# Transformer layer with a Strassen-type feed-forward: the gate row on the tensor engine, group results emptied in small pieces, first splits spread over a projection

## The chip, the core and the metric

The kernel runs on one core of a Trainium2 chip. The core has a tensor engine (PE in the profile; its weight loads are listed as PEld), a vector engine (DVE), a scalar engine (ACT), GpSimd (POOL) and a sync engine (SP). PE writes its sums to eight PSUM banks of 128 x 512 floats. SP and GpSimd each issue DMAs in their own order, and both share the core's 16 DMA engines. The metric is the device time of one launch in microseconds: 2732.56 us, the median of three runs (2732.09 to 2735.61).

## What is computed

One layer over 512 latent tokens of width 2048, all in fp32: an adaptive layer norm, one combined input projection, a recurrent and a windowed-attention group of heads, an output projection with a gated residual, and a SwiGLU feed-forward of width 5632 with a gated residual. What the change touches is the part from the output projection on:

```python
sh_m, sc_m, gt_m, sh_f, sc_f, gt_f = split(silu(c) @ w_mod + b_mod, 6)
x = x + gt_m * (concatenate([hg_lat, at_lat]) @ w_out)
h = modulate(rms_norm(x, norm_ffn_g), sh_f, sc_f)
gate, up = split(h @ w_gate_up, 2)
x = x + gt_f * ((silu(gate) * up) @ w_down)
```

`gt_f`, called the gate row below, is one row of 2048 numbers, a product of the vector `silu(c)` with a 2048 x 2048 block of `w_mod`, plus a bias. It is wanted only at the very end, where the feed-forward's result is scaled.

## The kernel before

**Products.** Every fp32 operand is split into a high part and a low part (`wh`/`wl` of a weight tile `wr`, `fh`/`fl` of a feed-forward tile `fx`, `mT` and `hT` with two parts each), and one product becomes three PE products, high x high, high x low and low x high (`mm3`). ACT makes the high part by a copy, DVE the low part by a subtraction, so each weight tile goes DMA, ACT, DVE, PE.

**Output projection.** `proj_a` multiplies eight 128-row pieces of the mixed heads (`mT`) with 512 columns of `w_out`, for the token tiles in `toks`, into one bank per token tile (`mm`); after each token tile of each pair of rows it calls `tick()`, and at the end `evac` (`add_gated`), which multiplies by the mixer's gate (`tm<-mm,gt_c` on DVE) and adds to `x`. There are two halves: rows of heads 8 to 15 first (`mT0`), for column blocks j = 0 to 3, then the other heads' rows (`mT1`), j = 0 to 3 again. In the second half the last block is done as two calls, tokens (0,1) and then (2,3). The mixed heads come through a DRAM buffer; `upto` loads them and splits them.

**Lanes.** `tick()` advances three lists of small tasks, which are so woven in between the projection's products: `lane` holds the remaining work on the recurrent heads (`gate_head`, whose last step per head is four PE transposes, `aux<-ident,gt`), and `mod_lane` holds four `mod_gate` tasks, one for each 512 numbers of the gate row. Each of them loads 4 MB of `w_mod` by SP in eight pieces (`m_w`), takes 16 DVE steps of multiply-and-add into `m_acc`, then one PE product of `m_acc` with ones (two passes), and writes 512 numbers to `gtf_d`. `lane.drain()` stands between the two halves and `mod_lane.drain()` after j = 2 of the second half: what is not done by then is done there, in a row. The order is fixed when the program is built; each engine runs its own list in that order.

**Feed-forward.** It runs as 22 groups of up products and 16 groups of down products, by a scheme of seven products for a 2 x 2 block product (`PRODUCTS`), with sums of blocks on both sides. A group has several steps (eight for up; for down `ENDS` says after which step each group ends, and a group goes on from the one four before it), a step has 42 PE products of 256 columns, and a group's seven results fill seven of the eight banks: p1, p2, p6, p7, q4, q5, p3 in that order. For each step DVE forms sums of the loaded weight blocks (`st_sums`, three instructions on `fx`), ACT copies the high part in two instructions (`fh`), and DVE subtracts for the low part (`st_low`, `fl`, 128 x 1792); all this is issued two steps ahead of the products. The first two steps' splits are made between the calls for tokens (0,1) and (2,3) of the projection. The first eight steps also turn the tokens into the left operand (`turn`, `form_sums`, `form_low`; the tiles `a`).

**Emptying a group.** `evac_up` and `evac_down` are generators, advanced at fixed places of the step loop. At a group's end ACT copies p1, DVE makes two sums with p2 and p6 (`big<-aux,big` and the like), then comes the next `st_low`, and then five sums in a row with p7, q4, q5, q5 and p3. The next group's products can go into a bank when the sum that reads it is done. `evac_up` later multiplies with SiLU, forms sums (`a_sums`), splits (`hl`) and stores the result to `sf_d` by GpSimd; the down groups read it back as `a`. For each of the last four down groups (b = `FIN`), GpSimd adds the DRAM partial result `y_d` by an accumulating DMA, DVE multiplies by the gate row's 512 numbers (`gtr`, one buffer, loaded by `prepare`), GpSimd adds `x1_d`, and the result goes out; for the last group the tile `z` holds that sum ready.

## Time and profile before

| what | value |
|---|---|
| median of three runs | 2732.56 us |
| the profiled execution | 2736.58 us, of which the trace's span is 2734.8 us |
| PE busy | 2535.5 us, 93% of the span |
| DVE busy | 2136.3 us, 78% |
| ACT busy | 1091.6 us, 40% |
| TensorE clock, mean share of full speed | 0.979 |
| DMA | 488.83 MB, 179 GB/s in the mean |

The stages, by PE's timeline: input projection and heads to about 1005 us; first half of the output projection to 1112.7; work on the heads until 1127.8; second half with j = 0, 1, 2 to 1201.0; the rest of the gate row to 1227.2; tokens (0,1) and (2,3) of j = 3 to 1258.8; norm and first turns to 1276.5; up products to about 2215; down products to 2705.2; the end, without PE, to 2734.8. PE is the busiest engine nearly everywhere, so the views to read are those of what PE waits for. All rows carry L131, the line of a helper that issues every instruction; work is told apart by its tiles, written out<-in. A row such as "1.54 <-DVE big" in brackets is idle time of the engine just before the instruction, and what ended it.

### The profile page before, as it was taken

Reading aid. Unit: us, or ns where it says so; the run is one execution under the profiler, and the core shown is the slowest. Engines: PE = TensorE matmul, PEld = TensorE weight load, DVE = VectorE, ACT = ScalarE, POOL = GpSimd, SP = SyncE. Lnnn points to the kernel's source line nnn. Section 1 sums busy time; section 2 is a strip of 40 time slices with the busy share of each in tenths; the row PEclk is TensorE's granted clock in tenths of the full one; section 3 lists DMA queues with packets and bytes.
Section 4 is the critical chain, followed back from the end, with each engine's and each line's share of the span. In section 5 each row is a group of like instructions: output and inputs, shape, how many; then the busy total and the mean of one; then the engine's idle time right before and its main releaser. Section 6 shows DMA issues by size and latency. Waiting matters only on the chain.

```text
span 2734.8 us, 44380 instructions
## 1 busy us (share of the span) xinstructions
PE 2535.5 (93%) x17119; PEld 2288.9 (84%) x17119; DVE 2136.3 (78%) x3666; ACT 1091.6 (40%) x1801; POOL 258.6 (9%) x448
## 2 busy tenths in 40 slices
PE   7999999999999999767999999999999989999994
PEld 4579888878788878556999999999999989999994
DVE  4478868787888876656888888888888887777775
ACT  4245444446333332224544444434444433333331
POOL 0000010000011110100000000000000022222201
PEclk9999999999999999888999999999999999999998
DMA  9978677751532354752344444454444486777766
GB/s 346 300 266 264 208 231 239 231 179 60 158 97 91 101 176 157 228 180 69 109 131 155 140 142 157 126 162 154 127 156 150 150 291 229 208 219 228 221 157 155
DMA packets 310165, 488.83 MB, mean 179 GB/s; under 512 B 20417, under 2 KB 177250, under 8 KB 309186
## 3 DMA queue, kind: packets, MB, share of 16 engines
q1 hardware_dynamic: 258528, 351.35, 40.5%
q0 software_dynamic: 38048, 122.00, 14.8%
q10 hardware_dynamic: 13378, 12.65, 1.4%
q8 instruction: 134, 2.20, 0.3%
q14 instruction: 77, 0.63, 0.1%
HBM read 414.08 MB, written 71.84 MB: 178 GB/s over the span
## 4 chain that ended last, share of the span: by engine, by line
DVE 29%; issue 26%; PE 23%; DMA 13%; ACT 7%; POOL 3%; SPq 0%; DVEq 0%; ACTq 0%; POOLq 0%
PE mm L131 17%; DVE fx L131 9%; PE aux L131 6%; DVE big L131 6%; DMA m_w<-in_w_mod_dram 5%; ACT fh L131 4%; DVE fl L131 4%; DVE m_acc L131 2%; DVE wl L131 2%; DMA wr<-in_w_in_dram 1%; DMA y_d<-big 1%; DMA big<-x_d 1%; DMA big<-y_d 1%; POOL a L131 1%; DVE hP L131 1%
## 5 line engine op out<-in xcount | busy, mean ns | idle before, releaser
L131 ACT ACTIVATE fh<-fx 128x768 fp32r<-128x768 f32 (+1 forms) x528 | 483.2, 946 | 814.5 <-DVE fx L131 747.8
L131 DVE TENSOR_TENSOR fl<-fx,fh 128x1792 fp32r<-128x1792 f32 x264 | 533.9, 2023 | 170.1 <-ACT fh L131 169.0
L131 PE MATMUL mm<-a,fh 128*128 128x256 f32 x2464 | 470.0, 283 | 12.4 <-DVE big L131 9.1
L131 PE MATMUL aux<-a,fh 128*128 128x256 f32 x2464 | 469.5, 283 | 10.3 <-DVE big L131 10.3
L131 DVE TENSOR_TENSOR fx<-fx 128x256 f32<-128x256 f32 (+1 forms) x816 | 417.4, 512 | 43.9 <-DMA fx<-in_w_down_dram 13.1
L131 PEld LDWEIGHTS mm<-a,fh 128*128 128x128 f32 x2464 | 381.2, 189 | 17.1 <-DVE big L131 8.3
L131 PEld LDWEIGHTS aux<-a,fh 128*128 128x128 f32 x2464 | 381.1, 189 | 14.8 <-DVE big L131 9.2
L131 ACT ACTIVATE wh<-wr 128x512 fp32r<-128x512 f32 x376 | 227.1, 627 | 307.6 <-PE mm L131 191.4
L131 PE MATMUL mm<-a,fl 128*128 128x256 f32 x1232 | 348.6, 283 | 0.0
L131 PE MATMUL aux<-a,fl 128*128 128x256 f32 x1232 | 348.4, 283 | 0.0
L131 DVE TENSOR_TENSOR wl<-wr,wh 128x512 fp32r<-128x512 f32 x376 | 250.4, 684 | 98.0 <-ACT wh L131 97.3
L131 PE MATMUL mm<-wh,hT 128*128 128x512 f32 x896 | 297.0, 400 | 4.1 <-ACT hT L131 3.0
L131 PE MATMUL aux<-fh,a 128*128 128x256 f32 x1232 | 267.5, 284 | 15.8 <-DVE big L131 15.6
L131 PE MATMUL mm<-fh,a 128*128 128x256 f32 x1232 | 267.4, 284 | 14.5 <-DVE big L131 13.4
L131 PE MATMUL mm<-hT,wh 128*128 128x512 f32 x768 | 248.3, 399 | 0.0
L131 DVE SCALAR_TENSOR_TENSOR m_acc<-m_w,c_col,m_acc 128x512 f32<-128x512 f32 x240 | 179.4, 747 | 66.5 <-DMA m_w<-in_w_mod_dram 64.1
L131 PEld LDWEIGHTS mm<-a,fl 128*128 128x128 f32 x1232 | 231.2, 188 | 0.0
L131 PEld LDWEIGHTS aux<-a,fl 128*128 128x128 f32 x1232 | 231.1, 188 | 0.0
L131 PEld LDWEIGHTS aux<-fh,a 128*128 128x128 f32 x1232 | 209.5, 190 | 20.0 <-DVE big L131 15.6
L131 PEld LDWEIGHTS mm<-fh,a 128*128 128x128 f32 x1232 | 209.3, 189 | 18.5 <-DVE big L131 13.1
L131 PEld LDWEIGHTS mm<-wh,hT 128*128 128x128 f32 x896 | 168.4, 188 | 55.5 <-issue 8.6
L131 PE MATMUL mm<-wh,mT 128*128 128x512 f32 x512 | 169.5, 408 | 15.5 <-DVE gsig L131 6.1
(274 smaller groups left out, 4110.1 us busy)
## 6 DMA issues: line engine op xcount, KB each, us to landing
fx<-in_w_gate_up_dram SPq DMA_DIRECT2D x352, 256.0 KB, 3.3
wr<-in_w_in_dram SPq DMA_DIRECT2D x144, 512.0 KB, 4.3
m_w<-in_w_mod_dram SPq DMA_DIRECT2D x128, 512.0 KB, 4.6
fx<-in_w_down_dram SPq DMA_DIRECT2D x176, 256.0 KB, 6.1
sf_d<-big POOLq DMA_DIRECT2D x44, 896.0 KB, 6.0
ring<-in_w_mod_dram SPq DMA_DIRECT2D x64, 512.0 KB, 8.8
a<-sf_d POOLq DMA_DIRECT2D x44, 512.0 KB, 10.3
wr<-in_w_out_dram SPq DMA_DIRECT2D x36, 512.0 KB, 4.5
```

The source lines that it names most:

```text
L131: r = f(*a, **k)
```

## The change

**1. The gate row by PE.** The four `mod_gate` tasks are gone. A row tile `c_pad` with `silu(c)` in the first of 32 columns is the stationary operand; `gate_rows(k)`, for k = 0 to 15, multiplies it with a 128 x 2048 block of `w_mod` (`gw`, 1 MB, three buffers, loaded on GpSimd's queue) by four column-tiled products of 32 x 512, all into one bank. Four of these stand in j = 2, four in the call for tokens (0,1), three in that for (2,3), and five behind it; then one DVE addition of the bias and four small writes to `gtf_d`.

**2. Emptying in small pieces.** Pieces of at most three instructions stand between `st_sums` and `st_low`, where before they stood behind `st_low`. The sum with p3 comes one step later than those with q4 and q5, and these come after the next step's `st_sums`. The low part of a step is made in two instructions where no emptying is under way. The movements after a down group are in a list of their own (`moves`); `prepare(j + 1)` is called as soon as the one buffer of `gtr` is free, and `z` is loaded at the start of the last group.

**3. First splits spread.** `st_sums`, `st_high` and `st_low` of the first two steps stand at several places inside the calls for (0,1) and (2,3).

**4. `ENDS`** gives the last groups 5, 5, 8, 7, 6 and 5 steps in place of 6, 6, 8, 7, 5 and 4.

The core of the diff:

```diff
-ENDS = (2, 3, 5, 6, 8, 9, 11, 12, 14, 15, 17, 18, 22, 22, 22, 22)
+ENDS = (2, 3, 5, 6, 8, 9, 11, 12, 14, 15, 16, 17, 22, 22, 22, 22)
...
-    for j in range(4):
-        mod_lane.add(mod_gate(j, 5 * D, gtf_d))
...
-    def st_low(i):
+    def st_low(i, parted=False):
...
+            for a, b in ((0, 3), (3, 7)) if parted else ((0, 7),):
+                dve.tensor_tensor(u.lo[:, a:b, :], u.x[:, 1 + a:1 + b, :], u.hi.bitcast(F32)[:, a:b, :],
+                                  op=ALU.subtract)
...
+    def gate_load(k):
+        if k < KC:
+            gws[k] = est.tile(gw, [P, D], F32, "gw", "gw", 3)
+            pool.dma_start(gws[k], w_mod[k * P:(k + 1) * P, 5 * D:6 * D])
+
+    def gate_rows(k):
+        if k == 0:
+            pg.append(aux_bank())
+        w = gws.pop(k)
+        for j in range(4):
+            pe.matmul(pg[0][32 * j:32 * j + 32, :], c_pad[:, k, :], w[:, 512 * j:512 * j + 512], start=(k == 0),
+                      stop=(k == KC - 1), tile_position=(0, 32 * j), skip_group_check=True)
+        gate_load(k + 3)
...
+            if j == 2:
+                gate_rows(s // 2)
...
-    mod_lane.drain()
...
-    proj_a(ws, list(range(8)), mT, (0, 1), 512, last)
-    for i in range(2):
-        st_sums(i)
-        st_high(i)
-    for i in range(2):
-        st_low(i)
-    proj_a(ws, list(range(8)), mT, (2, 3), 512, last)
+    def before(s):
+        gate_rows(4 + s // 2)
+        if s == 2:
+            st_sums(0)
+            st_high(0)
+        if s == 4:
+            st_low(0)
+        if s == 6:
+            st_sums(1)
+            st_high(1)
+
+    proj_a(ws, list(range(8)), mT, (0, 1), 512, last, before)
+
+    def before(s):
+        if s > 0:
+            gate_rows(7 + s // 2)
+        if s == 0:
+            st_low(1)
+
+    proj_a(ws, list(range(8)), mT, (2, 3), 512, last, before)
+    for k in range(11, KC):
+        gate_rows(k)
...
+    dve.tensor_tensor(g_row, pg[0], g_row, op=ALU.add)
+    for j in range(4):
+        pool.dma_start(gtf_d[0:1, 512 * j:512 * j + 512], g_row[32 * j:32 * j + 1, :])
...
         dve.tensor_tensor(t, r, p7, op=ALU.subtract)
+        yield
         dve.tensor_tensor(u1, t, q4, op=ALU.add)
+        dve.tensor_tensor(t, q5, t, op=ALU.subtract)
         dve.tensor_tensor(r, q5, r, op=ALU.subtract)
-        dve.tensor_tensor(t, q5, t, op=ALU.subtract)
+        act.activation(t, t, AF.Silu)
+        yield
+        xx = est.tile(xg, [P, 8, SC], F32, "big", "big", 4)
         dve.tensor_tensor(r, p3, r, op=ALU.add)
...
+    def move(j, b, c, gt):
+
...
         dve.tensor_tensor(c, c, gt[:, None, :].to_broadcast([P, 4, 512]), op=ALU.mult)
+        prepare(j + 1)
         pool.dma_start(c, rows_of(x1_d, j), accum_op=ALU.add)
...
+        advance(tail)
+        if not u.up and u.b == 0 and u.g < 2:
+            advance(tail)
+        st_low(i + 2, not tail and not g)
...
         if g:
-            next(g, None)
+            next(g)
             tail.append(g)
+        advance(moves)
```

What this makes of the engines' lists. PE, before: the place where the two halves of the output projection meet (`mT_9843` and `mT_9844` are parts of the first half, `mT_10824` of the second).

```order
L131 MATMUL mm<-wl,mT_9843 128x512
L131 MATMUL mm<-wh,mT_9844 128x512
L131 MATMUL aux<-ident,gt 128x128 x12
L131 MATMUL aux<-m_acc,ones 128x512
L131 MATMUL mm<-wh,mT_10824 128x512
L131 MATMUL mm<-wl,mT_10824 128x512
```

PE, after, at the same place (the second half is `mT_10763` and `mT_10764` here).

```order
L131 MATMUL mm<-wl,mT_9843 128x512
L131 MATMUL mm<-wh,mT_9844 128x512
L131 MATMUL mm<-wh,mT_10763 128x512
L131 MATMUL mm<-wl,mT_10763 128x512
L131 MATMUL mm<-wh,mT_10764 128x512
```

The twelve transposes of the last three heads and the product of `m_acc` no longer stand between the halves: the transposes stand as fours inside the first half, the last of them some 20 rows ahead of its end.

GpSimd's DMA list, after, from j = 2 to the end of the projection (`x_d` is the store of one finished block of x, 1 MB; `gw` the loads for the gate row; before, the only other entries here are loads and writes of the gate row's bias and result).

```order
L131 DMA x_d<-x_9833 128x4x512
L131 DMA gw<-in_w_mod_dram 128x2048 x3
L131 DMA x_d<-x_9834 128x4x512
L131 DMA gw<-in_w_mod_dram 128x2048 x7
L131 DMA x_d<-x_9835 128x4x512
L131 DMA gw<-in_w_mod_dram 128x2048 x2
L131 DMA gtf_d<-g_row 16x1x32 x4
```

The last two loads of the gate row stand behind the store of the last block of x, and the writes of the finished row behind them. On PE five groups of column-tiled products (`aux<-gw,c_pad_10777`, twenty in a row) now stand between the projection's last product and the first turn.

DVE, before, at the end of an up group: sums of the next weights, two sums with p2 and p6, low part, then p7, q4, q5, q5 and p3.

```order
L131 TENSOR_TENSOR fx<-fx 128x512
L131 TENSOR_TENSOR fx<-fx 128x256 x2
L131 TENSOR_TENSOR big<-aux,big 128x512
L131 TENSOR_TENSOR big<-mm,big 128x512
L131 TENSOR_TENSOR fl<-fx,fh 128x1792
L131 TENSOR_TENSOR big<-big,aux 128x512
L131 TENSOR_TENSOR big<-big,mm 128x512
L131 TENSOR_TENSOR big<-aux,big 128x512 x2
L131 TENSOR_TENSOR big<-mm,big 128x512
```

DVE, after, at the same place.

```order
L131 TENSOR_TENSOR big<-aux,big 128x512
L131 TENSOR_TENSOR big<-mm,big 128x512
L131 TENSOR_TENSOR fl<-fx,fh 128x1792
L131 TENSOR_TENSOR big<-big,aux 128x512
L131 TENSOR_TENSOR fx<-fx 128x512
L131 TENSOR_TENSOR fx<-fx 128x256 x2
L131 TENSOR_TENSOR big<-big,mm 128x512
L131 TENSOR_TENSOR big<-aux,big 128x512 x2
L131 TENSOR_TENSOR fl<-fx,fh 128x1792
```

The sums with q4 and q5 now stand behind the next step's sums of weights and ahead of its low part; the sum with p3 has moved one step further.

## Rows read from the trace of the kernel before

**Rows 1.** Stretches: us, then busy us (instructions) of PE, PEld, DVE, ACT, POOL; clock; DMA.

```profile
1020.00:1030.00 10.00, 10.00 (x44) 8.04 (x44) 7.05 (x14) 3.08 (x6) 0.88 (x2) 1.00 1.05 371
1113.00:1128.00 15.00, 4.26 (x15) 2.25 (x16) 10.41 (x17) 3.20 (x6) 1.88 (x3) 0.66 0.66 216
1153.00:1160.00 7.00, 5.66 (x15) 4.00 (x15) 6.96 (x12) 2.48 (x6) 0.00 (x0) 0.58 0.58 172
1160.00:1201.00 41.00, 41.00 (x179) 33.68 (x178) 18.98 (x29) 12.96 (x28) 1.54 (x2) 0.99 0.50 165
1201.00:1227.00 26.00, 1.91 (x4) 0.69 (x3) 14.62 (x21) 3.63 (x9) 1.87 (x3) 0.58 0.67 214
1227.00:1266.00 39.00, 26.09 (x98) 19.86 (x96) 24.74 (x47) 12.12 (x22) 1.31 (x2) 0.85 0.27 93
```

**Rows 2.** PE's waits from 1000 to 1280: total us, times, longest.

```profile
PE aux L131 <- DVE m_acc L131: 24.1, 1, 24.1
PE aux L131 <- DVE gt L131: 9.8, 3, 7.5
...
PE mm L131 <- DVE tm L131: 4.4, 2, 3.3
```

**Rows 3.** PE's timeline around one group of column-tiled products, early in the kernel.

```profile
120.59 0.63 PE L131 MATMUL mm<-wh,hT 128*128 128x512 f32 x2
121.15 1.06 PE L131 MATMUL aux<-ring,c_pad 128*32 128x512 f32 x8
122.14 0.50 PE L131 MATMUL mm<-wl,hT 128*128 128x512 f32 x1
```

**Rows 4.** DVE's timeline around the end of one up group.

```profile
1502.32 1.60 DVE L131 TENSOR_TENSOR fx<-fx 128x512 f32<-128x512 f32 x3
...
1505.59 2.02 DVE L131 TENSOR_TENSOR fl<-fx,fh 128x1792 fp32r<-128x1792 f32 x1
1507.52 0.68 DVE L131 TENSOR_TENSOR big<-big,aux 128x512 f32<-128x512 f32 x1
1508.30 0.69 DVE L131 TENSOR_TENSOR big<-big,mm 128x512 f32<-128x512 f32 x1
...
1510.70 1.60 DVE L131 TENSOR_TENSOR fx<-fx 128x512 f32<-128x512 f32 x3
1513.43 2.03 DVE L131 TENSOR_TENSOR fl<-fx,fh 128x1792 fp32r<-128x1792 f32 x1 [1.13 <-ACT fh L131]
```

**Rows 5.** The same table of stretches, for the up and the down products.

```profile
1340.00:2200.00 860.00, 840.75 (x6908) 832.28 (x6909) 750.94 (x929) 363.53 (x412) 48.91 (x53) 1.00 0.47 148
2200.00:2700.00 500.00, 463.85 (x3781) 454.89 (x3779) 390.94 (x479) 175.59 (x198) 109.27 (x138) 0.99 0.73 215
```

**Rows 6.** Waits of PE and of DVE from 1340 to 2200.

```profile
PE aux L131 <- DVE big L131: 10.3, 22, 0.9
PE mm L131 <- DVE big L131: 9.1, 21, 0.6
...
DVE fl L131 <- ACT fh L131: 91.3, 81, 1.1
```

**Rows 7.** PE's waits from 2200 to 2700.

```profile
PE aux L131 <- DVE big L131: 15.6, 17, 2.8
PE mm L131 <- DVE big L131: 13.4, 17, 1.6
```

**Rows 8.** The last PE product, and DVE's and GpSimd's timelines behind it.

```profile
2704.96 0.28 PE L131 MATMUL aux<-fh,a 128*128 128x256 f32 x1
...
2712.12 2.90 DVE L131 TENSOR_TENSOR big<-big,gtr 128x2048 f32<-128x2048 f32 x2 [6.82 <-DMA gtr<-gtf_d]
2723.32 0.69 DVE L131 TENSOR_TENSOR big<-big 128x512 f32<-128x512 f32 x1 [8.31 <-DMA big<-x_d]
...
2702.01 1.08 POOL L131 DMA_DIRECT2D gtr<-gtf_d  x1
...
2714.83 1.30 POOL L131 DMA_DIRECT2D big<-x_d  x1 [4.77 <-DVE big L131]
```

More of the change, by code (lines that the diff above doesn't have):

```diff
@@ L1459, in tile_block @@
                       op=ALU.mult)
+    dve.tensor_tensor(g_row, pg[0], g_row, op=ALU.add)
+    for j in range(4):
+        pool.dma_start(gtf_d[0:1, 512 * j:512 * j + 512], g_row[32 * j:32 * j + 1, :])
+    m_st.close()
+    r_st.close()
+    asets = ctx.enter_context(tc.tile_pool(name="asets", bufs=1, side="right"))
     sets, xa = {}, {}
@@ L1482, in form_sums @@
         if s < 8:
-            a_sums(xa[s])
+            for _ in a_sums(xa[s]):
+                pass
             act.activation(sets[s][0][:, 0:3, :], xa[s][:, 1:4, :], AF.Copy)
@@ L1520, in evac_up @@
         yield
-        dve.tensor_tensor(hl[1], xx[:, 1:8, :], hl[0].bitcast(F32), op=ALU.subtract)
-        for i in range(2):
+        for i, (a, b) in enumerate(((0, 3), (3, 7))):
+            dve.tensor_tensor(hl[1][:, a:b, :], xx[:, 1 + a:1 + b, :], hl[0].bitcast(F32)[:, a:b, :],
+                              op=ALU.subtract)
             pool.dma_start(sf_d[2 * g + i].bitcast(F32).rearrange("f p n -> p f n"), hl[i].bitcast(F32))
@@ L1533, in prepare @@
     def prepare(j):
+        gt = est.tile(fx, [P, 512], F32, "gtr", "gtr", 1)
+        pool.dma_start(gt, gtf_d[0:1, 512 * j:512 * j + 512].to_broadcast([P, 512]))
         z = None
         if j == 3:
[L1537 to L1545 removed]
+            z = zs[0]
             dve.tensor_tensor(z, z, gt[:, None, :].to_broadcast([P, 4, 512]), op=ALU.mult)
             pool.dma_start(z, rows_of(x1_d, j), accum_op=ALU.add)
[L1548 removed]
+        prepared[j] = gt, z
+    zs = []
     prepared = {}
@@ L1569, in evac_down @@
         yield
+        dve.tensor_tensor(t, r, p7, op=ALU.subtract)
         done(0, 1)
-        dve.tensor_tensor(t, r, p7, op=ALU.subtract)
+        yield
         dve.tensor_tensor(c21, t, q4, op=ALU.add)
+        done(1, 1)
+        dve.tensor_tensor(t, q5, t, op=ALU.subtract)
         dve.tensor_tensor(r, q5, r, op=ALU.subtract)
-        dve.tensor_tensor(t, q5, t, op=ALU.subtract)
+        done(1, 0)
+        yield
         dve.tensor_tensor(r, p3, r, op=ALU.add)
-        for h, n in ((0, 0), (1, 1), (1, 0)):
-            done(h, n)
-        if z is not None:
-            return
+        done(0, 0)
+        if z is None:
+            moves.append(move(j, b, c, gt))
+        yield
+    def move(j, b, c, gt):
         if b < FIN:
@@ L1637, in tile_block, with advance @@
         turn(s, 1)
-    form_sums(0)
-    form_low(0)
-    form_sums(1)
-    form_low(1)
-    tail = []
+    for s in range(2):
+        form_sums(s)
+        form_low(s)
+    tail, moves = [], []
+    def advance(gens):
+        for x in list(gens):
+            if next(x, gens) is gens:
+                gens.remove(x)
     for i, u in enumerate(steps):
@@ L1658, in tile_block @@
             next(g)
-        for x in list(tail):
-            if next(x, tail) is tail:
-                tail.remove(x)
-        st_low(i + 2)
+        advance(tail)
+        if not u.up and u.b == 0 and u.g < 2:
+            advance(tail)
+        st_low(i + 2, not tail and not g)
         if i < 8:
@@ L1665, in tile_block @@
         if g:
-            next(g, None)
+            next(g)
             tail.append(g)
+        advance(moves)
         if not u.up and u.b == FIN and u.first:
-            tail.append(prepare(u.g))
+            if u.g == 0:
+                prepare(0)
+            if u.g == 3:
+                zs.append(est.tile(xg, [P, 4, 512], F32, "big", "big", 4))
+                pool.dma_start(zs[0], rows_of(y_d, 3))
         reload(i)
-    while tail:
-        for x in list(tail):
-            if next(x, tail) is tail:
-                tail.remove(x)
+    while tail or moves:
+        advance(tail)
+        advance(moves)
 _INS = ["x", "c", "ctx", "c_ctx", "w_mod", "b_mod", "norm_mix_g", "norm_ffn_g", "w_in", "hg_lb",
```

37 lines of the change are left out of this document (18 added, 19 removed).

## The prediction

> **What bounds the kernel now.** I read the page's first part, then the table of stretches, then PE's waits in each stretch, and then the timeline of the engine that PE waits for. PE is busy in 93% of the span, so only its idle time and its slow time can be won. The stretches show where these are. Between the halves of the output projection PE works 4.26 of 15 us, in the rest of the gate row 1.91 of 26 us [rows 1]; the one is work on the last heads (DVE `gt`, 9.8 us of waits), the other one wait of 24.1 us for `m_acc` [rows 2]. In the up products PE works 840.75 of 860 us, in the down products 463.85 of 500 [rows 5]; nearly all that is missing are waits for the sums that free its banks, 10.3 + 9.1 us [rows 6] and 15.6 + 13.4 us [rows 7]. Behind the last product stand 30 us without PE.
>
> Why the banks come late is seen on DVE. In an ordinary step of the loop its three sums start at 1510.70, the low part at 1513.43, after a wait of 1.13 us for ACT's high part, and a low part takes 1.94: 4.67 us. At a group's end the same two and seven sums take from 1502.32 to 1510.70, 8.38 us [rows 4]. So DVE needs 8.38 + 7 x 4.67 = 41.1 us for an up group, and more where later pieces exceed the 1.13 us. PE's product takes 840.75/6908 = 0.122 us [rows 5], a group of 8 x 42 of them 40.9 us. DVE is a little slower than PE: it has no lead, and what stands last in its row is late at each group's end, by 19.4 us in some 21 groups.
>
> **The sum is made against the profiled execution**, 2736.6 us (span 2734.8 and 1.8 outside it), which is 4.0 above the median; at the end 4.0 comes off.
>
> **1. Between the halves.** The head transposes now stand inside the first half. DVE loses some 36 us of `m_acc` steps in the two halves, so the heads' chain should come earlier; the three fours stand about 50 products (12 us) apart. Of the 15 us [rows 1] some 2 us stay: -13. Ends: -15, and -8 if the last head is still late by as much as its single longest wait, 7.5 us [rows 2]. One product of `m_acc` with ones goes from the first half: -1.
>
> **2. j = 0 to 2.** At the end of j = 0 PE waited 4.4 us for `tm` [rows 2], which stood behind an `m_acc` step waiting for its load, and ran at a clock of 0.58 after it: 15 products took 5.66 us [rows 1], where the later stretch has 41.00/179 = 0.229 each, so 2.2 us more. Both go: -6.6. Four gate groups come in. A group of the same shape takes 1.06 us, and from the last ordinary product (second of the pair from 120.59) to the next (122.14) pass 1.09 us more than the usual spacing [rows 3], with about 0.1 more behind it: 1.2 us. Four: +4.8.
>
> A rule that speaks against this part: the Trainium skill, TensorEngine Tiling (Array Packing), Tiling Modes, says that changing the tiling mode drains the engine, and here it is changed 24 times. The row has the drains in it and they are small, some 0.1 us on each side, 2.4 us in all. If each change emptied the engine for as long as the first product behind the group lasts, 0.50 us [rows 3], it would be 12 us, and the forecast 10 later; the row bears out the rule but not that size, and I keep the row's.
>
> **3. Rest of the gate row.** The stretch 1201 to 1227 goes, with its product and its cold clock: -26. Nothing else was drained there.
>
> **4. Tokens (0,1) and (2,3).** They took 31.8 us for 96 products, which at 0.229 are 22.0; 9.8 us were cold clock (0.85 [rows 1]) and waits for the first splits, which blocked the weight tiles' low parts on DVE. These go; seven gate groups add 8.4. The loads are tight: from the start of j = 2 to the last group some 24 MB have to come or go (13.6 of `gw`, 6 of weights, 3 of stores, 1.6 of `fx`) in about 74 us, 330 GB/s. The most seen in a 10 us stretch is 371 [rows 1]. I take 3 us of waits: +1.6 in all, ends -4 and +7.
>
> **5. Before the first turn.** The last product used to be followed after 7.4 us by the first turn. Now five gate groups come between, and their last two loads stand on GpSimd's queue behind the store of the last block of x, which waits for DVE's last addition, about 2.5 us after the last product. Then 3.1 MB are under way, 8.5 us at 371 GB/s, and some 2 us for landing and the group: 14 us instead of 7.4, +6.5 (ends +3, if the store leaves the loads room, and +12). The norm and `diag` lie beside it. The finished row's four small writes hold back the first `a` tile, which takes over their place in memory; I put that at nothing, since the first turns cover it, and up to +3 if not.
>
> **6. Up products.** DVE's new group: at the end 1502.32 to 1505.59 (3.27), the low part 1.93, the sum with p7 0.78: 5.98. Next step: sums 1.52, three sums at 0.6 (1508.30 to 1510.70 are four), low part 1.94: 5.3. All later pieces are at most two short sums and fit into the 1.13 us wait for ACT [rows 4, 6]. 5.98 + 5.3 + 6 x 4.67 = 39.3 us against PE's 40.9. So DVE gains 1.6 us a group until it leads by as much as its buffers allow; from then on PE should find each bank free, with little to spare at q5. The ceiling is the 19.4 us; the first groups, where the forming of `a` leaves no lead, keep some 4: -15. Ends -5 and -19. The second instruction of a parted low part costs 0.05 us, where DVE has time.
>
> **7. Down products.** A group of six steps: 5.98 + 5.3 + 4 x 4.67 = 30.0 us on DVE against 252 products at 0.122, 30.8, on PE. The gain of a group is half as large and groups of two or five steps have none, so the lead comes back more slowly: of 29.0 us of waits 24 go, ends -12 and -29. The other 7 idle us of that stretch I leave.
>
> **8. The end.** Before: the last product starts at 2704.96; `gtr` is asked for at 2702.01 and awaited until 2712.12; the sum with `x1_d`, asked for at 2714.83, is there at 2723.32 [rows 8], 18 us after PE, and 11.5 us of DVE work and the last store follow. Now the partial result for `z` is loaded a group ahead, and `gtr` is asked for when the product of the last-but-one group is done, which can be some 10 us before PE ends, since that group now ends five steps before it. With the same 10 us for `gtr`, 2.3 for the product and 8.5 for the sum, `x1_d` is in about 10 us after PE ends: -8, ends -3 and -11.
>
> **Sum.** -13 - 1 - 6.6 + 4.8 - 26 + 1.6 + 6.5 = -33.7 up to the first turn; -15 - 24 - 8 = -47 behind it. 2736.6 - 80.7 = 2655.9, less 4.0: **2652 us**.
>
> **Rivals.**
>
> *A. The loops gain nothing.* DVE's step is set by the round from sums to ACT to low part, and a piece between them may push ACT's work as well, since ACT runs SiLU and the split of the result in the same row. Then the new group is as long as the old one, the waits of [rows 6, 7] stay, and 39 us are missing: 2691. For it: ACT is what DVE waits for, 91.3 us in 81 waits [rows 6]. Against it: ACT has 363.5 of 860 us to do [rows 5].
>
> *B. Slower: the banks of q4 and q5 come later than now.* Their sums now stand behind the next step's three sums of weights, 1.52 us later in the row. If DVE gets no lead, each of some 37 groups waits longer by that, and the old waits stay: +56. 2736.6 - 33.7 - 8 + 56 - 4 = 2747. It decides from 42/37 = 1.1 us per group on. For it: DVE has no lead now, and the down groups end every 30 us with a spare of under 1 us. Against it: a wait of PE gives DVE the lead that it lacks, so the loss should be paid once and not in each group, as long as DVE's round is the shorter one.
>
> *C. The gate row's loads bound the projection.* They share the DMA engines with the weight tiles. At 290 GB/s in place of 330 the 24 MB take 84 us, +10, and weight tiles late in their turn would leave PE cold, some 4 more: 2666. For it: in the stretch of 26 us in which hardly anything but `m_w` was loaded, 214 GB/s went over [rows 1]; against it: there two buffers limited it.
>
> The Trainium skill, DMA: Bandwidth & Descriptors, Queues, rings and completion order, says that a DMA engine takes packets from its queues in turn; by that the loads on GpSimd's queue would take their share from SP's weight tiles whenever both are full, which is what C describes. No row here shows the two queues full at once.
>
> *D.* The order of the lists shows that the change is made as told; that a part of it doesn't take place is no case of its own.
>
> **Chances.** Forecast 60%, with its own range 2625 to 2675 (the ends of the steps, most of which will not fall on one side together: -27 and +23); A 14%, C 15%, B 8%, and 3% for a result near the old time by a mixture of A and B. A measurement of this kernel can tell some 0.2% from no change, 5.5 us. The range is to leave out B and the outer part of the others: 2622 to 2694. Faster 0.89, same 0.03, slower 0.08.
>
> **What would show it.** The wait of 24.1 us and the two idle stretches should be gone, and the clock stay near 1.00 from 1020 on until the last product of the projection. Right: 11 to 17 us there between that product and the first turn. In the up products PE's waits for `big` under 6 us in all and the interval of two group ends 40.9; in the down products under 8. If DVE's wait for `fh` stays at 91 us while the bank waits stay too, A holds; if the longest bank wait at q4 or q5 is near 2.5 us all along, B. If PE waits for `gw` or for `wh` in j = 2 and j = 3, C. What would make the forecast wrong most of all is DVE's lead: all of 6 and 7 rests on it.

## The result and the profile after

The changed kernel takes 2639.39 us (median of four runs, 2634.27 to 2641.55) against 2734.09 us: a ratio of 0.9649, 95% interval 0.963 to 0.9668, 95 us faster. 2652 us was forecast, with 2625 to 2675 as the forecast's own range. The way there differs from the forecast more than the sum does. The table sets the profiled executions' traces side by side, by PE's starts: the first product of the output projection, its last one, the first turn, the first up and the first down product, the last product, the end of the span.

| stretch, us | before | after | measured | forecast |
|---|---|---|---|---|
| start to the output projection | 1006.7 | 1001.8 | -4.9 | 0 |
| both halves of the projection, with what stood between | 251.6 | 222.9 | -28.7 | -40.2 |
| last product to first turn | 7.8 | 15.5 | +7.6 | +6.5 |
| turns | 7.3 | 5.5 | -1.8 | 0 |
| up products | 941.3 | 914.8 | -26.5 | -15 |
| down products | 492.1 | 456.1 | -36.0 | -24 |
| behind the last product | 27.8 | 23.1 | -4.7 | -8 |
| span | 2734.8 | 2639.8 | -95.0 | -80.7 |

The projection gave less than forecast, the loops more. The stretches of the changed kernel's projection, from j = 2 on, with the columns of [rows 1] (us, busy us and instructions of PE, PEld, DVE, ACT and POOL, clock, DMA share, GB/s):

```profile
1157.00:1184.00 27.00, 27.00 (x134) 18.50 (x136) 10.09 (x15) 7.10 (x16) 2.94 (x5) 1.00 0.86 303
1184.00:1203.00 19.00, 16.45 (x81) 9.15 (x74) 9.49 (x14) 7.03 (x15) 2.88 (x5) 1.00 0.74 275
1203.00:1226.00 23.00, 19.63 (x83) 10.39 (x87) 12.39 (x18) 7.45 (x15) 1.59 (x3) 0.85 0.67 235
1226.00:1240.00 14.00, 5.64 (x36) 0.67 (x28) 4.73 (x19) 0.80 (x3) 1.81 (x3) 0.64 0.67 252
```

PE is busy throughout j = 2, but in j = 3 (from 1184) it idles 2.6 and 3.4 us, the clock falls to 0.85 and then to 0.64. What it waits for from 1000 to 1280, as in [rows 2]:

```profile
PE aux L131 <- DMA gw<-in_w_mod_dram: 9.3, 4, 7.0
...
PE mm L131 <- ACT wh L131: 3.5, 2, 2.4
PE mm L131 <- DVE tm L131: 2.7, 3, 1.5
```

The wait of 24.1 us for `m_acc` and the waits for `gt` are gone. New are waits for the gate row's own loads and for the weight tiles' high parts. PE's and GpSimd's timelines at the end of the projection:

```profile
1225.10 1.92 PE L131 MATMUL aux<-gw,c_pad 128*32 128x512 f32 x16
...
1235.89 1.94 PE L131 MATMUL aux<-gw,c_pad 128*32 128x512 f32 x8 [7.03 <-DMA gw<-in_w_mod_dram]
1238.38 1.93 PE L131 MATMUL aux<-gw,c_pad 128*32 128x512 f32 x8 [0.55 <-DMA gw<-in_w_mod_dram]
1240.24 4.73 PE L131 MATMUL aux<-diag,x 128*128 128x128 f32 x40
...
1227.82 0.77 POOL L131 DMA_DIRECT2D x_d<-x  x1 [4.75 <-DVE x L131]
1228.59 1.05 POOL L131 DMA_DIRECT2D gw<-in_w_mod_dram  x2
```

The five groups behind the last product (the row of 16 at 1225.10 is two of them) wait for their last two loads, issued at 1228.59 behind the store of the last block of x at 1227.82; the first of the two is in at 1235.89, and a group takes 1.9 us there in place of 1.06, in a stretch with a clock of 0.64. The first turn starts at 1240.24.

In the loops the waits are turned round. DVE's waits from 1310 to 2170 in the changed kernel, to be set beside [rows 6]:

```profile
DVE big L131 <- PE aux L131: 20.5, 10, 2.0
DVE big L131 <- PE mm L131: 20.5, 10, 2.0
DVE fl L131 <- ACT fh L131: 16.6, 63, 0.3
```

DVE waits for PE, 41 us in 20 groups, where PE waited for DVE; and its wait for ACT has fallen from 91.3 to 16.6 us. One group's end on DVE, for [rows 4]:

```profile
1705.21 1.60 DVE L131 TENSOR_TENSOR fx<-fx 128x512 f32<-128x512 f32 x3
1707.03 2.17 DVE L131 TENSOR_TENSOR fl<-fx,fh 128x768 fp32r<-128x768 f32 x2 [0.21 <-ACT fh L131]
1709.12 1.61 DVE L131 TENSOR_TENSOR fx<-fx 128x512 f32<-128x512 f32 x3
1712.77 0.69 DVE L131 TENSOR_TENSOR big<-aux,big 128x512 f32<-128x512 f32 x1 [2.05 <-PE aux L131]
...
1714.18 2.02 DVE L131 TENSOR_TENSOR fl<-fx,fh 128x1792 fp32r<-128x1792 f32 x1
1716.11 0.68 DVE L131 TENSOR_TENSOR big<-big,aux 128x512 f32<-128x512 f32 x1
1716.71 1.60 DVE L131 TENSOR_TENSOR fx<-fx 128x512 f32<-128x512 f32 x3
```

The row at 1712.77 carries it: DVE has reached the group's end 2.05 us before PE's result is there. PE's period of a group is 336 products at 200.00/1665 us, 40.4 us, so DVE's round, the time that its work for one group takes without waits for PE, is 38.3. The lines of the same 200 us stretch, before and then after:

```profile
1700.00:1900.00 200.00, 195.53 (x1608) 193.50 (x1607) 174.26 (x217) 83.84 (x97) 7.83 (x8) 1.00 0.45 141
```

```profile
1700.00:1900.00 200.00, 200.00 (x1665) 199.78 (x1664) 181.96 (x235) 91.00 (x100) 9.91 (x10) 1.00 0.48 148
```

Before, 57 products fewer (6.8 us at 0.120 each) were done in 200 us, though PE was idle for only 4.5. In this stretch the breaks cost PE about half as much again as the idle time that the trace shows; PE's starts, one group to the next, stood 41.8 us apart and stand 40.4 apart now. This is why the loops gained more than the waits in [rows 6, 7] promise.

The end, PE, DVE and GpSimd in the changed kernel, and PE's last row of before:

```profile
2616.70 0.28 PE L131 MATMUL aux<-fh,a 128*128 128x256 f32 x1
...
2616.02 2.29 DVE L131 TENSOR_TENSOR big<-big,gtr 128x2048 f32<-128x2048 f32 x1 [3.83 <-DMA gtr<-gtf_d]
...
2627.39 0.69 DVE L131 TENSOR_TENSOR big<-big 128x512 f32<-128x512 f32 x1 [6.29 <-DMA big<-x_d]
...
2612.48 0.57 POOL L131 DMA_DIRECT2D gtr<-gtf_d  x1 [10.75 <-DVE big L131]
```

```profile
2706.96 0.28 PE L131 MATMUL aux<-fh,a 128*128 128x256 f32 x1
```

`x1_d` is in at 2627.39, 10.7 us after the last product. Before, the last product starts at 2706.96 and not at 2704.96: the row in [rows 8] (and the end of the down products in the list of stages) is not the kernel's last, and the sum was in 16.4 us after the last one, not 18.

### The profile page after: what moved, and what is told of

Same layout as the page of the kernel before. It is cut to its first block, busy times and chain, and to the rows that moved or that the text cites. A ratio compares the mean times of both kernels' runs of the same rounds, so it can differ in the third digit from the quotient of the medians.

```text
span 2639.8 us, 44545 instructions
## 1 busy us (share of the span) xinstructions
PE 2531.1 (96%) x17239; PEld 2282.7 (86%) x17239; DVE 2105.6 (80%) x3691; ACT 1110.5 (42%) x1801; POOL 265.7 (10%) x466
## 4 chain that ended last, share of the span: by engine, by line
PE 68%; DVE 11%; DMA 10%; issue 6%; ACT 2%; POOL 1%; SPq 0%; DVEq 0%; ACTq 0%; POOLq 0%
PE mm L131 40%; PE aux L131 28%; DMA m_w<-in_w_mod_dram 3%; DVE big L131 2%; DVE m_acc L131 2%; DVE wl L131 2%; DVE fx L131 1%; DMA wr<-in_w_in_dram 1%; DMA fx<-in_w_down_dram 1%; DMA big<-x_d 1%; DVE fl L131 1%; DVE ce L131 1%; DMA gw<-in_w_mod_dram 1%; DVE a L131 1%; POOL rs_t L131 1%
## 5 line engine op out<-in xcount | busy, mean ns | idle before, releaser
L131 ACT ACTIVATE fh<-fx 128x768 fp32r<-128x768 f32 (+1 forms) x528 | 500.2, 952 | 734.5 <-DVE fx L131 209.8
L131 DVE TENSOR_TENSOR fl<-fx,fh 128x1792 fp32r<-128x1792 f32 (+2 forms) x333 | 543.8, 1635 | 36.3 <-ACT fh L131 34.6
L131 PE MATMUL mm<-wh,mT 128*128 128x512 f32 x512 | 171.4, 406 | 10.7 <-DVE gsig L131 4.0
L131 PE MATMUL mm<-wl,hT 128*128 128x512 f32 x448 | 179.5, 401 | 0.3 <-DVE wl L131 0.3
```

The lines of the kernel that those rows point to most:

```text
L131: r = f(*a, **k)
```

## The experiments

In all of them the comparison is with the kernel before, on the same chip. Kernels that share the projection's code differ there by up to 5 us from trace to trace (221.5 to 226.4), and in the start by up to 6 (995.8 to 1001.8); the up and the down products of kernels that share the loops repeat within 2.3. Inside the projection j = 3 is steadier: from its first to its last product of `mT` it takes 39.9 to 40.0 us in the six kernels that have it as in the changed one. The stretches of all traces, as above:

| kernel | to projection | projection | to turn | turns | up | down | end | span |
|---|---|---|---|---|---|---|---|---|
| before | 1006.7 | 251.6 | 7.8 | 7.3 | 941.3 | 492.1 | 27.8 | 2734.8 |
| after | 1001.8 | 222.9 | 15.5 | 5.5 | 914.8 | 456.1 | 23.1 | 2639.8 |
| loops only | 1005.1 | 249.2 | 7.9 | 7.6 | 914.5 | 454.6 | 22.9 | 2661.7 |
| projection only | 998.5 | 226.3 | 15.1 | 5.4 | 941.1 | 493.1 | 26.1 | 2705.5 |
| early q | 998.1 | 224.0 | 15.5 | 6.4 | 912.8 | 458.1 | 21.3 | 2636.2 |
| dose of 8 | 997.6 | 226.4 | 15.2 | 5.4 | 944.9 | 455.5 | 22.5 | 2667.6 |
| gate without loads | 996.3 | 218.0 | 7.7 | 7.0 | 914.4 | 454.8 | 22.9 | 2621.2 |
| gate earlier by four | 999.8 | 229.8 | 7.6 | 7.8 | 914.5 | 455.7 | 23.2 | 2638.5 |
| first splits at once | 995.8 | 231.3 | 15.5 | 6.3 | 916.7 | 454.8 | 22.4 | 2642.8 |
| low parts parted only | 1006.3 | 250.2 | 7.9 | 7.6 | 911.7 | 479.3 | 26.0 | 2689.0 |
| no parting | 999.1 | 221.9 | 15.5 | 6.5 | 915.3 | 459.2 | 23.1 | 2640.5 |
| old row at the end | 1001.2 | 221.5 | 15.5 | 6.3 | 914.7 | 468.4 | 21.6 | 2649.1 |
| gate first | 998.0 | 224.0 | 7.6 | 7.5 | 914.9 | 453.8 | 23.3 | 2629.1 |
| gate first, early fx | 999.4 | 223.8 | 7.6 | 7.0 | 914.5 | 454.6 | 22.4 | 2629.3 |

### Do the parts add?

"Loops only" puts the projection, the lanes and the first splits back to the kernel before and keeps the new emptying, `moves` and `ENDS`; "projection only" is the reverse.

```diff
 # loops only, against the changed kernel
+    for j in range(4):
+        mod_lane.add(mod_gate(j, 5 * D, gtf_d))
...
-                gate_rows(s // 2)
...
+    proj_a(ws, list(range(8)), mT, (0, 1), 512, last)
+    for i in range(2):
+        st_sums(i)
+        st_high(i)
```

> The projection, the gate row and the first splits are as in the kernel before; the emptying in pieces and the new group lengths are as in the changed kernel. Theory (DVE's shorter round makes the loops PE-bound by itself): from the first product of the up phase on it takes what the changed kernel takes there (26.5 us less in the up products, 36.0 less in the down products, 4.7 less at the end), so about 2667 us; bank waits of PE in the up products under 5 us. Rival (the loops gained because the projection left them a better start, a hot clock and early loads): half of that or less, 2700 us or more.

2663.78 us (2660.85 to 2665.39), ratio 0.9756 (0.9729 to 0.9784).

> The gate row by PE and the spread first splits are as in the changed kernel, the loops as in the kernel before. If the two parts add, this is 26 to 28 us faster than before, about 2706 us, with bank waits of 19 us in the up products and 29 in the down products as before. Rival (the loops also gain from what the projection leaves): 2690 us or less.

2705.80 us (2702.39 to 2708.13), ratio 0.9911 (0.9882 to 0.9939). Within that spread each stretch takes in either kernel what it takes in its parent, and the two gains, 64 and 22 us on their chip, add to 86, which their intervals, some 7 us to either side each, don't tell from 95. The loops do not gain from what the projection leaves.

### Is it DVE's round against PE's?

A dose of work on DVE, and nothing else:

```diff
         st_low(i + 2, not tail and not g)
+        if 8 <= i < 8 * N_UP:
+            v = steps[i + 2]
+            dve.tensor_tensor(v.lo[:, 6, :], v.x[:, 7, :], v.hi.bitcast(F32)[:, 6, :], op=ALU.subtract)
```

> The changed kernel with one further DVE subtraction of 128 x 256 (0.43 us alone, some 0.38 in a row) behind the low part of every step of the up phase, repeating a part of it. Theory (DVE's round of 39.3 us against PE's 40.4): 8 x 0.38 makes it 42.3, so each up group takes about 2 us more, 40 to 50 us slower in all and PE's bank waits are back. Rival (DVE has much more slack than that, the loops are bound by buffers or by ACT): under 15 us slower.

2667.46 us (2662.03 to 2669.36), ratio 0.9768 (0.9739 to 0.9797). The up products take 30.1 us more, less than the 40 to 50 that were expected and far more than the rival's 15 at most. DVE's timeline in this kernel, for the size of the dose, and PE's waits from 1700 to 2100:

```profile
1707.53 2.49 DVE L131 TENSOR_TENSOR fl<-fx,fh 128x1792 fp32r<-128x1792 f32 x2 [0.33 <-ACT fh L131]
1709.93 1.60 DVE L131 TENSOR_TENSOR fx<-fx 128x512 f32<-128x512 f32 x3
```

```profile
PE mm L131 <- DVE big L131: 5.1, 9, 0.6
PE aux L131 <- DVE big L131: 5.0, 9, 0.6
```

A low part with the dose takes from 1707.53 to 1709.93, 2.40 where it took 1.94: 0.46 a step, 3.7 a group. On top of the measured round of 38.3 that is 42.0, against 40.36 + 30.1/21 = 41.8 us measured. So the theory holds, and what was off was my 39.3 for the round, of which the expectation still made use. PE's bank waits are back at the size of before.

"Early q" takes the other direction: fewer pieces.

```diff
         dve.tensor_tensor(t, r, p7, op=ALU.subtract)
-        yield
         dve.tensor_tensor(u1, t, q4, op=ALU.add)
```

> The changed kernel, but the sums with q4 and q5 stand directly behind the sum with p7, ahead of the next step's sums of weights; only p3 and what follows is in pieces. Theory (what counts is DVE's round per group, against PE's 40.4 us): the three sums no longer fall into the wait for ACT, DVE's up group grows from 39.3 to about 40.5 us, so the lead is just lost: 0 to 12 us slower, most in the down products where groups are shorter. Rival B of the prediction (late banks of q4 and q5 cost time): some us faster than the changed kernel, with fewer bank waits.

2637.91 us (2629.30 to 2640.03), ratio 0.9655 (0.9618 to 0.9692): no difference. DVE's waits for PE from 1310 to 2156:

```profile
DVE big L131 <- PE aux L131: 13.6, 10, 1.4
DVE big L131 <- PE mm L131: 11.9, 9, 1.4
```

DVE still has some 1.3 us to spare in a group, where the changed kernel has 2.05. So the old place of the sums with q4 and q5 costs DVE 0.7 us a group and PE nothing. That is the net of two things, since the emptying then ends a step earlier and two of a group's low parts are parted in place of one. Rival B, that these sums come too late behind the next sums of weights, is not borne out, and neither does it help to put them there.

### Which edit of the loops does it?

The kernel before with nothing but the parted low part:

```diff
-        st_low(i + 2)
+        st_low(i + 2, not tail and not g)
```

> The kernel before with one edit: the low part of a step in two instructions where no emptying is under way. Theory (the first instruction needs only the first part of ACT's copy, so DVE's wait of 1.13 us shrinks to some 0.3 and such a step takes 3.9 instead of 4.67 us): one such step per up group, DVE's round 42.1 - 0.8 = 41.3 against PE's 40.4, so the bank waits fall by about a half, 12 to 18 us; two or three such steps in a down group of six, which makes those groups PE-bound, 12 to 20 us. Together about 2703 us. Rival (the prediction's: it costs 0.05 us a step and brings nothing): 2730 to 2740 us.

2686.27 us (2680.21 to 2690.79), ratio 0.9833 (0.9816 to 0.9849): 44 us, nearly half of the whole change, and all of its gain in the up products (911.7). DVE's timeline in this kernel, a step with a whole low part and a step with a parted one:

```profile
1725.00 2.02 DVE L131 TENSOR_TENSOR fl<-fx,fh 128x1792 fp32r<-128x1792 f32 x1 [1.13 <-ACT fh L131]
1726.94 1.60 DVE L131 TENSOR_TENSOR fx<-fx 128x512 f32<-128x512 f32 x3
1728.47 0.95 DVE L131 TENSOR_TENSOR fl<-fx,fh 128x768 fp32r<-128x768 f32 x1
1729.68 1.23 DVE L131 TENSOR_TENSOR fl<-fx,fh 128x1024 fp32r<-128x1024 f32 x1 [0.26 <-ACT fh L131]
1730.82 1.61 DVE L131 TENSOR_TENSOR fx<-fx 128x512 f32<-128x512 f32 x3
```

The whole one waits 1.13 us for ACT's second copy. The parted one starts its first piece, which needs only ACT's first copy, at once, and waits 0.26 us ahead of the second: the step takes 3.88 in place of 4.67 us. Two of a group's eight steps are so; 1.6 us a group bring DVE's round from the 41.8 of before down to PE's 40.4. I had expected one such step and half of the waits to stay.

The reverse, the changed kernel without the parting (`st_low(i + 2)` in the loop):

> The changed kernel, but every low part is one instruction, as before. Theory (in the up phase either the pieces or the parted low part gives DVE its lead; DVE's round is then 38.3 + 0.8 = 39.1 us against 40.4): the up products stay at 914 to 917 us. In the down products some of the steps lose 0.8 us each and the groups of two and five steps fall behind: 456 to 464 us. 0 to 9 us slower in all. Rival (as the parted low part alone brought the whole gain in the up products, it is the cause, and the pieces bring nothing): up products at 930 us or more.

2641.79 us (2637.60 to 2647.63), ratio 0.9672 (0.9644 to 0.9700). The up products stay at 915.3; DVE's waits for PE from 1310 to 2158 are

```profile
DVE big L131 <- PE mm L131: 12.5, 10, 1.3
DVE big L131 <- PE aux L131: 12.5, 10, 1.3
```

25 us in 20 groups in place of 41. So in the up products the pieces alone suffice, and the parting alone suffices. In the down products they don't: parting alone gives 479.3, the pieces without it 459.2, both 456.1, of 492.1. Beside the pieces, then, the parting is worth some 3 us in the down products, and the times of the two kernels (0.9672 and 0.9649) have intervals that overlap.

Then the row at the group's end put back, with all else kept:

```diff
         dve.tensor_tensor(t, r, p7, op=ALU.subtract)
-        yield
         dve.tensor_tensor(u1, t, q4, op=ALU.add)
...
+        dve.tensor_tensor(r, p3, r, op=ALU.add)
+        yield
...
-        yield
-        dve.tensor_tensor(r, p3, r, op=ALU.add)
```

> The changed kernel, but at a group's end all five sums with p7, q4, q5, q5 and p3 stand in a row behind the low part, as before; what comes later stays in pieces. Theory (DVE's round decides, 38.3 + 2.1 = 40.4 us against 40.4 in an up group): the up products 0 to 8 us longer. In the down products the kernel with parted low parts alone kept the old row and lost 23 us more than the changed one; if that is from this row, down products of 470 to 480 us here. Rival (that came from the movements after a group, the early load of the gate row's part and the lengths of the last groups): 456 to 462 us.

2649.74 us (2644.94 to 2651.91), ratio 0.9698 (0.9676 to 0.9720). Up products 914.7, with DVE's idle time all used up; down products 468.4, between theory and rival. PE's bank waits from 2160 to 2627:

```profile
PE aux L131 <- DVE big L131: 9.9, 12, 3.8
PE mm L131 <- DVE big L131: 9.3, 13, 1.4
```

Of the 36 us in the down products some 12 come from the row at the group's end. Between "parted only" (479.3) and this kernel lie another 11. What is left for them are the later pieces ahead of the low part, the movements in their own list, the earlier loads of `gtr` and `z` and the group lengths; no run separates these.

### What do the gate row's loads cost?

The same products, with only the first three blocks loaded:

```diff
-        w = gws.pop(k)
+        w = gws[k % 3]
...
-        gate_load(k + 3)
```

> The changed kernel, but only the first three 1 MB blocks for the gate row are loaded and used again and again: 13 of the 16 loads, 13.6 MB, are left out (the gate row is then a wrong one), all PE products stay. Theory (the 10 us that j = 3 takes longer than before, and the wait before the first turn, come from these loads): the stretch of j = 3 falls by some 8 us, the way from its last product to the first turn from 15.5 to about 8, 2625 us in all. Rival (it is the products themselves and the clock): under 4 us faster.

2622.50 us (2618.71 to 2623.01), ratio 0.9603 (0.9589 to 0.9618). The way to the first turn is 7.7 us again, though the same five groups stand in it: without waits they fit beside the norm. The projection takes 218.0, about 5 us less than with the loads. In j = 3 it takes 34.7 us (1179.59 to 1214.32) against 40.9 in the changed kernel, so 6 us there are from loads; the granted clock is 1.00 throughout that stretch, where it was 0.85 from 1203 on with the loads. The other end of the same fact is the time that a weight tile of `w_out` needs to land: from 1200 to 1262 before, from 1184 to 1240 after, and from 1180 to 1235 without the loads (the issues' row: engine, count, KB each, median us from issue to landing):

```profile
wr<-in_w_out_dram SPq DMA_DIRECT2D x4, 512.0 KB, 3.8
```

```profile
wr<-in_w_out_dram SPq DMA_DIRECT2D x4, 512.0 KB, 11.9
```

```profile
wr<-in_w_out_dram SPq DMA_DIRECT2D x4, 512.0 KB, 4.3
```

The groups moved ahead by four places, none behind the projection:

```diff
-            if j == 2:
-                gate_rows(s // 2)
+            if j > 0:
+                gate_rows(4 * (j - 1) + s // 2)
...
-        gate_rows(4 + s // 2)
+        gate_rows(8 + s // 2)
...
-    for k in range(11, KC):
-        gate_rows(k)
```

> The changed kernel with the gate groups moved ahead by four: k = 0 to 3 in j = 1, 4 to 7 in j = 2, 8 to 11 in the call for tokens (0,1), 12 to 15 in that for (2,3), none behind the projection; the loads move with them. Theory (the loads have room in j = 1, where the trace shows 141 GB/s): the first turn follows the last product after about 8 us instead of 15.5, j = 3 takes no longer than now, 6 to 12 us faster. Rival (the queue is full at any place, the waits only move): within 3 us of the changed kernel.

2635.21 us (2629.56 to 2640.29), ratio 0.9652 (0.9635 to 0.9670): not to be told from the changed kernel. The way to the turn fell by 7.9 us and the projection grew by some 6 to 7. Nearly all of that are the five more groups inside it, 5.9 us of products that used to stand beside the norm. The loads still meet the weight tiles (12.7 us to land), and PE's waits for their high parts from 1105 to 1245 are 4.9 us in place of 3.5.

Moved further ahead, to j = 0, 1 and 2, with the last three blocks lying ready in the buffers:

```diff
-            if j == 2:
-                gate_rows(s // 2)
+            gate_rows(4 * j + s // 2)
...
-    for k in range(11, KC):
+    for k in range(13, KC):
         gate_rows(k)
```

> The changed kernel with the gate groups moved ahead: k = 0 to 3 in j = 0, 4 to 7 in j = 1, 8 to 11 in j = 2, 12 at the start of the call for tokens (0,1), and only 13 to 15, whose blocks then lie ready in the three buffers, behind the projection. Theory (the price left is that of loads that meet the weight tiles of j = 3 and the store of the last block): no load of the gate row is issued after the first part of (0,1), j = 3 without waits for weight tiles, first turn some 8 us after the last product: 8 to 11 us faster than the changed kernel, about 2629 us. Rival (as when they were moved by four, the loads only meet other weight tiles in j = 0 to 2): within 3 us.

2634.03 us (2630.93 to 2639.71), ratio 0.9645 (0.9622 to 0.9668). The three groups stand in the shadow of the norm:

```profile
1222.34 2.78 PE L131 MATMUL aux<-gw,c_pad 128*32 128x512 f32 x24
1229.62 6.84 PE L131 MATMUL aux<-diag,x 128*128 128x128 f32 x40 [4.49 <-issue]
```

Projection and turn together take 231.6 us against 238.4, and the trace's span is 10.7 us shorter, of which 3.8 lie ahead of the projection. The times of the runs don't tell the two kernels apart (0.9645 against 0.9649).

The theory's "j = 3 without waits" did not come. The weight tiles land in 4.5 us again, and yet PE waits 4.8 us for high parts there, and the granted clock falls to 0.80:

```profile
1205.00:1222.00 17.00, 14.14 (x44) 10.58 (x45) 9.79 (x14) 5.37 (x12) 0.00 (x0) 0.80 0.09 31
```

The stretch of j = 3, from its first to its last product of `mT`, takes 33.8 us here, with no gate group in between, and 33.7 us in the kernel without the loads, with six groups in between and at a clock of 1.00. So once their loads are out of the way, the groups' products cost next to nothing in j = 3, where PE waits anyway; moved ahead, into j = 0 and 1, they cost 1.17 us each.

The same with the first weight tiles of the feed-forward loaded in j = 1:

```diff
+            if j == 1 and s > 0:
+                st_load(s // 2 - 1)
...
-    for i in range(3):
-        st_load(i)
```

> The changed kernel with the gate groups moved ahead as in the run before this one (four each in j = 0, 1 and 2, one in the call for (0,1), three behind the projection), and the first three feed-forward weight tiles (1.5 MB) loaded in j = 1 in place of after j = 2, so that they are out of the way of the weight tiles of j = 3. Theory (what PE still waits for in j = 3, 4.8 us on ACT's high part, is weight tiles that come late beside other loads): those waits fall by half, 2 to 4 us faster than the gate groups moved alone, 8 to 14 us faster than the changed kernel, about 2628 us. Rival (the weight tiles' own ring sets it, each load waits for its buffer): no change to the run before.

2634.58 us (2627.49 to 2640.94), ratio 0.9638 (0.9615 to 0.9661): no change to the run before. PE's wait for the high parts from 1100 to 1245 is what it was:

```profile
PE mm L131 <- ACT wh L131: 4.9, 4, 1.8
```

So these 4.9 us are not from the `fx` loads. That the ring of weight tiles sets them is the rival's reading, and the trace speaks against it for the most part. Here is the longest of the four waits, with ACT's rows ahead of it:

```profile
1205.56 1.06 ACT L131 ACTIVATE fh<-fx 128x1024 fp32r<-128x1024 f32 x1 [1.54 <-DVE fx L131]
1206.52 1.14 ACT L131 ACTIVATE wh<-wr 128x512 fp32r<-128x512 f32 x2
...
1207.19 0.51 PE L131 MATMUL mm<-wh,mT 128*128 128x512 f32 x1 [1.82 <-ACT wh L131]
```

At none of the four waits does ACT itself wait for a load just before. Each time its copy of the weight tile stands behind work that waited for DVE: twice behind the first splits (`fh`, 1.6 us for DVE's sums), twice behind the emptying of a block (`tm`, 1.5 us for DVE's addition). In this stretch ACT waits for a load only once, 2.99 us, ahead of the splits before the longest wait. No run changes ACT's order alone, so this is read from the trace and not shown.

### The first splits

All at once between (0,1) and (2,3), as before the change, the rest kept:

```diff
-        if s == 2:
-            st_sums(0)
-            st_high(0)
...
+    for i in range(2):
+        st_sums(i)
+        st_high(i)
+    for i in range(2):
+        st_low(i)
     proj_a(ws, list(range(8)), mT, (2, 3), 512, last, before)
```

> The changed kernel, but the first two steps' sums, high and low parts stand all at once between the calls for tokens (0,1) and (2,3), as before the change. Theory of the prediction (there they hold up the weight tiles' low parts): 4 to 8 us slower. Rival (in the changed kernel the weight tiles are late because of their loads, not of DVE): within 3 us.

2645.55 us (2643.23 to 2654.91), ratio 0.9697 (0.9678 to 0.9717). The projection takes 231.3 us, some 7 more than its relatives. PE's wait, and ACT's row ahead of it:

```profile
1212.21 0.79 PE L131 MATMUL mm<-wh,mT 128*128 128x512 f32 x1 [7.62 <-ACT wh L131]
...
1208.07 3.57 ACT L131 ACTIVATE fh<-fx 128x768 fp32r<-128x768 f32 x4
1211.54 2.70 ACT L131 ACTIVATE wh<-wr 128x512 fp32r<-128x512 f32 x5
```

The four instructions for the first steps' high parts, 3.5 us, stand on ACT ahead of those of the weight tiles, behind the emptying of tokens (0,1), and PE waits 7.62 us for one. The theory named DVE's low parts; for these PE waits 1.91 us, after the wait for ACT. Spread, the splits save the projection some 7 us.

## Why the prediction was right, and where its steps failed

The sum is 14 us off. The steps by themselves, as the table of stretches has them, are off by 46 us if each is counted without its sign: the projection gave 11.5 us less than forecast, the loops 23.5 more. So the mechanisms of the loops and of the gate row were right, but that the time came this close is partly luck.

**1, between the halves: right.** From the first half's start to the second's PE took 121.1 us and takes 107.8 (1001.84 to 1109.66), -13.3 against -14.

**Ahead of it: a term was missing.** The start is 5 us shorter in this trace, and in the traces of all eleven kernels with the new gate row it is 995.8 to 1001.8 against 1005.1 to 1006.7 in the three with the old one. The first of the four old tasks ran already at 692 us, and PE waited behind it:

```profile
734.79 0.50 PE L131 MATMUL mm<-hT,wl 128*128 128x512 f32 x1 [1.81 <-DVE wl L131]
```

The 40 products of `hT` around this wait, from 725.5 us on, take 11.25 us, and 9.16 in the changed kernel, so 2.1 us are found here; where the rest comes from stays open. I had read PE's waits from 1000 on only.

**2, j = 0 to 2: +1.0 in place of -1.8.** The gate groups are priced rightly: they stand 6.67 us apart (1157.18, 1163.85), and 24 products at 0.229 between them are 5.50, so 1.17 us each, tiling changes included; the 10 us that longer drains would have added are not there. The two waits for `tm` at the end of j = 0, 4.4 us, are gone as forecast. But 2.7 us of new ones have come at the start of the second half, where, by DVE's timeline, the last banks of the first half are emptied in between the splits of the second half's first rows; with the halves moved together, the second seems to meet that work; no run tests it.

**3, the rest of the gate row: right,** 26.2 us.

**4, tokens (0,1) and (2,3): the largest miss in the projection.** They take 41.3 us where 33.2 were forecast (31.6 before, and 1.6), outside the ends that I gave. The products are as priced. Without the loads the stretch, measured to the end of its last product as here, takes 35.1 us, so the loads cost 6 us, which I had put at 3. The other 5 us of the miss are not from loads: 96 products and seven groups make 30.2 us, and 4.9 more remain without any load of `gw`. I had let all 9.8 us of cold clock and waits go with the old place of the first splits, and half of them stayed. The sign that I had named, a clock near 1.00 to the projection's end, failed by the loads: 0.85 from 1203 to 1226, and 1.00 without them. The condition of rival C, that the loads hold up the weight tiles of j = 3, came true, with some 4 of its 14 us: 3 here and 1 behind the last product. The trace of before had no row with both queues full; now the weight tiles land in 11.9 us where they landed in 3.8, and in 4.3 with the loads left out. The rule that I cited beside C, from the Trainium skill, DMA: Bandwidth & Descriptors, Queues, rings and completion order (engines take packets from their queues in turn), fits that number.

**5, before the first turn: right,** +7.6 against +6.5, and shown to be the loads: 7.7 us without them. By the timeline it is the last two, for the first of which PE waits 7.03 us.

**6, up products: the mechanism was right, the term too small, and one edit was judged wrongly.** The forecast had DVE's new round at 39.3 and PE's at 40.9 us, hence a lead and no waits. Measured: 38.3 and 40.4. The end step takes 5.5 where I had 5.98 (1709.12 to 1716.71, less the wait for PE), and one step in eight is parted and takes 3.9. The parted low part I had put at a cost of 0.05 us; it saves 0.8 wherever it is used, and alone would have given the whole gain of the up products. And the ceiling of 19.4 us, read from PE's idle time, was none: each us of idle time cost 1.5 in the stretch shown. My price of a product, 0.122, held that loss in it; it is 0.120 where PE runs through.

**7, down products: the same.** 36.0 against 24, above the upper end of 29, but not by the waits for banks alone: these fell from 29.0 to 9.8 us, by less than the 24 forecast, and not under the 8 that I had named as the sign. I had PE's round from rows with its breaks in them, and left the idle time that was not waits for banks, nearly all of which went too: PE's idle time in the whole stretch fell from 38.3 to 10.0 us. The other 8 us are loss beyond the idle time, as in the up products.

**8, the end: too large.** After as forecast (10.7 us from the last product to the sum with `x1_d`), but before was misread: the last product started 2 us later than the row that I used, so 2 us of the 8 were never there, and the work behind the sum takes 12.4 us in place of 11.5. The 10.7 itself has two misses in it that cancel: `gtr` is asked for 4.2 us ahead of the last product, not some 10, and is in after 3.5 us, not 10.

**The rivals.** A (no gain in the loops) and B (late banks) did not come: the dose shows that DVE's round decides, "early q" that the place of the sums with q4 and q5 does not. C came in part.

## What to carry to other kernels

Where a second engine waits in each step for the other half of a first engine's work, cut its instruction where that work is cut: this alone, without any reordering, gave 44 us here, where the whole change gave 95; beside the reordering, which frees the same engine by another way, it gave little more. What a stall costs is read from the products done in a stretch with and without stalls, not from idle time alone. And a saving on one queue is to be sought again in the transfers that share the engines with it: the gate row's 16 MB cost nothing on DVE any more, but 14 us of PE's time, 6 where the loads met the weight tiles and 8 where PE waited for the last two. And products moved out of a stretch that waits anyway are no saving.

## What the runs showed of the hardware

- Short waits of PE cost more than their idle time: 4.5 us idle in 200 us at a clock of 1.00, 6.8 us of products missing.
- A group of four column-tiled fp32 products of 32 x 512 among full ones costs 1.17 us, all changes of tiling included.
- Weight tiles of 512 KB on one queue land in 11.9 us while 1 MB loads run on the other, and in 4.3 us in the same kernel without those loads.
